# An encoder layer on one core: features-major x in the first FFN, and the weight sums of a seven-product form made partly by adding DMA transfers

## The chip, the cores and the metric

The kernel runs on one core of a Trainium2 chip. The metric is device microseconds (us) of one launch, the median of three runs. A core has TensorE (PE in the profile's rows, its weight loads PEld), VectorE (DVE), ScalarE (ACT), GpSimd (POOL) and SyncE (SP), which issues most DMA transfers. GpSimd can issue transfers too.

## What is computed

One layer of an encoder: an FFN, a token mixer (windowed attention and HGRN2), a second FFN, with a layer norm after each. There are 768 tokens (512 and 256) of 1024 features, all in float32. The two FFNs, called a and b here, are where the change lies:

```python
def swiglu_ffn(x, w13, w2):
    gate, up = jnp.split(x @ w13, 2, axis=-1)
    return (jax.nn.silu(gate) * up) @ w2
...
x = layer_norm(ALPHA * x + 0.5 * swiglu_ffn(x, ffn_w13[l, 0], ffn_w2[l, 0]), ln_g[l, 0], ln_b[l, 0])
x = layer_norm(ALPHA * x + mix, ln_g[l, 1], ln_b[l, 1])
x = layer_norm(ALPHA * x + 0.5 * swiglu_ffn(x, ffn_w13[l, 1], ffn_w2[l, 1]), ln_g[l, 2], ln_b[l, 2])
```

Each FFN has 2 x 2816 columns in w13, so 11 pairs of 256 gate columns and 11 pairs of 256 up columns.

## The kernel before

Every float32 operand of a product is split into two float32r parts, hi and lo (`split`, L111 to L113: ScalarE rounds the source to hi, VectorE subtracts hi from the source and gives lo). A product is then three matmuls: hi hi, hi lo, lo hi.

The first product of an FFN, w13 against x, is done in pairs of two 128-column tiles, by a seven-product form (a Strassen-Winograd form; the comment at L233 writes it out). The weights of a pair are four blocks A11, A12, A21, A22 (two halves of the features, two column tiles), x is four blocks B11, B12, B21, B22 (two token halves, two halves of the features). Seven products, each 4 x 3 = 12 matmuls of 384 tokens, take four sums S1 to S4 of weight blocks and four sums T1 to T4 of x blocks. S sums are made for each pair (`pair_weights`, L334), T sums once for each FFN (`form_sums`, L254).

x lies token-major in the tile `xr`. The products need it feature-major, so `turned` (L179) transposes 128 x 128 blocks on TensorE against an identity, into PSUM, and splits from there. FFN a does this for the four blocks of x (`form_base`) and for T1 to T4: 48 and 48 transposes.

The first gate pair is done in the plain form (`first_pairs`, L460 and `plain`, L466): 96 matmuls, which need only the four blocks of x, while T1 to T4 and the weights of the first up pair are made. From then on the loop at L497 goes through 11 steps of a gate pair and an up pair. Between products `fill` puts groups of six matmuls of the second product (w2, tile `pd`, L446). Their results are added to `xr` by VectorE (L450).

Buffers decide how far ahead things run. `ring` holds the split weight blocks: 6 tiles, so a block of the next pair is split as soon as a product has read one of the present pair. `raw` holds weights as they were loaded: 4 tiles, two for a pair, two for w2. SP issues loads in program order and waits at each for its tile to be free:

```python
def pair_load(w, c0, n):
    return load(col_unit(w, c0, 256, 4 * n, 4)).rearrange("p (k c) -> p k c", k=4)
```

In the order in which a scheduler puts each engine's instructions, every engine runs its own list strictly from the front: an instruction that waits holds up all behind it on that engine.

## Time and profile before

| | |
|---|---|
| median of three runs | 1485.89 us (1484.82 to 1486.19) |
| profiled execution: its span, first to last instruction (the page gives no other time of it) | 1483.4 us |
| TensorE, VectorE, ScalarE, GpSimd busy | 98%, 68%, 42%, 4% |
| instructions of TensorE / VectorE / ScalarE / GpSimd | 9439 / 1708 / 1226 / 68 |
| moved by DMA | 104.62 MB, mean 71 GB/s |
| granted TensorE clock, mean | 0.997 (of 2.4 GHz) |

A matmul's busy time overlaps that of the next one: twelve matmuls of 384 columns that each show 336 ns start 0.17 us apart. So a span of TensorE is read from starts, not from busy times. The page's percentage for TensorE tells that it hardly ever stands still, not how fast it goes.

### The profile page before, as it was taken

How to read it: one execution, taken by the hardware profiler on the slowest of the kernel's cores; microseconds unless marked ns; L12 is line 12 of the kernel's file. 1: busy time of each engine (PE TensorE's matmuls, PEld its weight loads, DVE VectorE, ACT ScalarE, POOL GpSimd, SP SyncE). 2: the span in 40 equal slices, each digit the busy share in tenths (PEclk: the TensorE clock that was granted, in tenths of full speed). 3: DMA queues.
4: the chain of work that ended last, by engine and by line, in shares of the span. 5: the costliest groups of instructions: out<-in, count | busy, mean ns of one | idle time of the engine just before them, and what ended most of it. 6: DMA issues, size and time to landing. Idle time of an engine off the chain costs nothing.

```text
span 1483.4 us, 23172 instructions
## 1 busy us (share of the span) xinstructions
PE 1454.8 (98%) x9439; PEld 1349.2 (91%) x9439; DVE 1010.3 (68%) x1708; ACT 617.3 (42%) x1226; POOL 52.7 (4%) x68
## 2 busy tenths in 40 slices
PE   8999999999999999999999999999999999999996
PEld 7999999999999888999988997899999999999995
DVE  7876677766777668444588746786777666777656
ACT  5543333333334444465664332363333324333341
POOL 1000000000000110000000001110000000000003
PEclk9999999999999999999999999999999999999999
DMA  6130222202212341211111042111212112122122
GB/s 200 58 100 31 85 77 67 85 29 86 86 57 86 105 114 44 72 30 30 29 45 44 17 142 100 43 60 54 86 57 86 56 59 86 60 84 70 45 71 86
DMA packets 86827, 104.62 MB, mean 71 GB/s; under 512 B 11816, under 2 KB 75712, under 8 KB 86720
## 3 DMA queue, kind: packets, MB, share of 16 engines
q1 hardware_dynamic: 86720, 103.14, 21.8%
q8 instruction: 74, 1.21, 0.4%
q14 instruction: 33, 0.27, 0.1%
HBM read 96.83 MB, written 6.29 MB: 70 GB/s over the span
## 4 chain that ended last, share of the span: by engine, by line
PE 89%; DVE 5%; ACT 2%; POOL 1%; issue 1%; DMA 1%; SPq 0%; DVEq 0%; ACTq 0%; POOLq 0%
PE pa L382 29%; PE pd L446 21%; PE pb L382 12%; PE pa L159 9%; PE ptm L609 5%; PE pwo L965 3%; PE pp L844 2%; PE pa L475 2%; PE ptr L183 1%; PE pav L738 1%; DVE xr L315 1%; PE plv L651 1%; ACT Ft L297 1%; PE ps L828 1%; PE pp L838 1%
## 5 line engine op out<-in xcount | busy, mean ns | idle before, releaser
L382 PE MATMUL pa<-areaA,ring 128*128 128x384 f32 x1488 | 274.1, 336 | 0.0
L382 PEld LDWEIGHTS pa<-areaA,ring 128*128 128x128 f32 x1488 | 260.8, 188 | 6.0
L113 DVE TENSOR_TENSOR ring<-raw,ring 128x512 fp32r<-128x512 f32 (+1 forms) x159 | 127.9, 807 | 88.5 <-ACT ring L112 84.6
L382 PE MATMUL pa<-areaB,ring 128*128 128x384 f32 x984 | 185.4, 337 | 0.0
L112 ACT CAST ring<-raw 128x512 fp32r<-128x512 f32 (+1 forms) x159 | 112.5, 710 | 174.7 <-PE pa L382 77.0
L446 PE MATMUL pd<-kc,Kt 128*128 128x512 f32 x720 | 185.1, 392 | 0.0
L382 PEld LDWEIGHTS pa<-areaB,ring 128*128 128x128 f32 x984 | 174.0, 188 | 6.0
L450 DVE SCALAR_TENSOR_TENSOR xr<-pd,xr 128x512 f32<-128x512 f32 x240 | 164.5, 686 | 6.2 <-PE pd L446 6.0
L159 PE MATMUL pa<-areaA,ring 128*128 128x384 f32 x864 | 167.5, 343 | 0.9 <-ACT Kt L628 0.8
L446 PEld LDWEIGHTS pd<-kc,Kt 128*128 128x128 f32 x720 | 133.7, 188 | 21.1
L159 PEld LDWEIGHTS pa<-areaA,ring 128*128 128x128 f32 x864 | 148.3, 188 | 2.5 <-ACT Kt L628 1.4
L112 ACT CAST ring<-P 128x512 fp32r<-128x512 f32 x80 | 49.8, 622 | 180.0 <-DVE Ft L352 51.2
L113 DVE TENSOR_TENSOR ring<-P,ring 128x512 fp32r<-128x512 f32 x80 | 55.3, 692 | 88.5 <-ACT ring L112 85.9
L446 PE MATMUL pd<-P,Kt 128*128 128x512 f32 x360 | 103.1, 394 | 1.0 <-DVE xr L450 1.0
L446 PE MATMUL pd<-Xt,Kt 128*128 128x512 f32 x360 | 102.4, 392 | 0.0
L382 PE MATMUL pb<-areaB,ring 128*128 128x384 f32 x480 | 91.2, 339 | 0.0
L382 PE MATMUL pb<-areaA,ring 128*128 128x384 f32 x480 | 89.8, 335 | 0.0
L382 PEld LDWEIGHTS pb<-areaB,ring 128*128 128x128 f32 x480 | 85.6, 188 | 3.1
L382 PEld LDWEIGHTS pb<-areaA,ring 128*128 128x128 f32 x480 | 84.5, 188 | 3.2
L609 PE MATMUL ptm<-ring,areaA 128*128 128x256 f32 x576 | 81.7, 289 | 0.0
L446 PEld LDWEIGHTS pd<-Xt,Kt 128*128 128x128 f32 x360 | 67.6, 188 | 15.1
L609 PEld LDWEIGHTS ptm<-ring,areaA 128*128 128x128 f32 x576 | 72.7, 191 | 0.5
(226 smaller groups left out, 2005.9 us busy)
## 6 DMA issues: line engine op xcount, KB each, us to landing
raw<-ffn_w SPq DMA_DIRECT2D x132, 512.0 KB, 4.1
raw<-w_in SPq DMA_DIRECT2D x22, 512.0 KB, 3.8
raw<-w_out SPq DMA_DIRECT2D x8, 512.0 KB, 3.4
park<-xr SPq DMA_DIRECT2D x6, 512.0 KB, 2.6
xr<-park SPq DMA_DIRECT2D x6, 512.0 KB, 6.3
raw<-w_in SPq DMA_DIRECT2D x8, 256.0 KB, 4.2
y_sample<-xr SPq DMA_DIRECT2D x4, 512.0 KB, 2.6
xr<-x_sample SPq DMA_DIRECT2D x6, 256.0 KB, 5.7
```

Of the source, the lines that this page charges most:

```text
L112: act.copy(dst_hi, src)
L113: dve.tensor_tensor(dst_lo, src, dst_hi.bitcast(F32), ALU.subtract)
L159: pe.matmul(pt, lhsT=hl[wi][:, k * P:(k + 1) * P], rhs=tri(g * 2048 + xi * 1024 + k * P), start=n == 0, stop=n == 3 * KT - 1)
L183: pe.transpose(pt[:, k * P:(k + 1) * P], src[:, k * P:(k + 1) * P], ident)
L297: act.activation(junk[c], x[c], AF.Square, bias=nm, accum_out=w[:, 2 + c:3 + c])
L382: pe.matmul(bank, lhsT=ws[b][:, wi, k, :], rhs=view(tl, off + xi * 512 + k * P, [[dist, 3], [1, P]]), start=n == 0 and not more, stop=n == ...
L446: pe.matmul(pd, lhsT=hT[f][:, hi * T + t * P:hi * T + (t + 1) * P], rhs=w[wi], start=n == 0, stop=n == tot - 1)
L450: dve.scalar_tensor_tensor(xs, pd, 0.5, xs, ALU.mult, ALU.add, accum_out=total)
L475: pe.matmul(bank, lhsT=w[:, k, m * P:(m + 1) * P], rhs=view(tl, off + xi * 512 + k * P, [[dist, 3], [1, P]]), start=i == 0, stop=i == 23)
L609: pe.matmul(pt, lhsT=xT(t, xi, k), rhs=w[k // 4][wi][:, k % 4, :], start=n == 0, stop=n == 3 * KT - 1)
L844: pe.matmul(pp[j][:, 384:448], lhsT=PTs[j % 2][:, i * P:(i + 1) * P], rhs=V[:, kb0 + i, kv * 64:kv * 64 + 64], start=i == 0, stop=i == nk - 1)
L965: pe.matmul(po[c], lhsT=cat(t, xi, k), rhs=wo[k][wi][c], start=k == 0 and n == 0, stop=k == KT - 1 and n == 2)
```

## The change

There are three parts.

**x of FFN a comes feature-major.** Besides x itself the kernel gets `x_t`, the same numbers with features on the partitions, a layout made outside (`_layouts`). `first_a` replaces `first_pairs` for FFN a. It loads x and the first weights in small steps (19 transfers ahead of all others), splits them straight from SBUF, and makes the T sums on VectorE from the untransposed blocks, 1536 elements at a time. No transposes are left in FFN a. The token-major `xr` is still loaded, for the residual, after all that. FFN b keeps `first_pairs`, `turned` and its transposes.

**Signs.** The second column tile of a pair is computed with its sign turned, so that every S sum is an addition: S1 = A21 + A22, S3 = A11 + A21, S2 = S1 + A11, S4 = S2 + A12. The T sums change sign accordingly, and the sign is undone in Silu (`scale=-1.0`) and in the product of gate and up (a multiplication by -1 within the same instruction).

**S1 and S3 by DMA.** w13 comes in another layout too (`w13_t`: for each pair and partition the blocks A22, A11, A12, A21 side by side, 2 KB each). For a pair, SP loads A22, A11, A12 into a new buffer `xb` (two tiles of 768 KB) and A22, A11 once more into a `raw` tile; GpSimd then issues two transfers that add A21 to both halves of that tile, which makes S1 and S3 in place. VectorE makes only S2 and S4. GpSimd's transfers wait for SP's load.

```diff
-    def pair_load(w, c0, n):
-        return load(col_unit(w, c0, 256, 4 * n, 4)).rearrange("p (k c) -> p k c", k=4)
-    def pair_loads(w, c0):
-        return [pair_load(w, c0, n) for n in range(2)]
+    def pair_loads(idx, j):
+        w = a["w13_t"][idx, j]
+        base = buf("xb").rearrange("p (b k c) -> p b k c", b=3, k=4)
+        nc.sync.dma_start(base, w[:, :3])
+        sums = raw_tile().rearrange("p (b k c) -> p b k c", b=2, k=4)
+        nc.sync.dma_start(sums, w[:, :2])
+        for b in range(2):
+            nc.gpsimd.dma_start(sums[:, b], w[:, 3], accum_op=ALU.add)
+        return [base[:, b] for b in range(3)] + [sums[:, b] for b in range(2)]
...
         def s2():
-            diff(1, A21, A22, ALU.add)
-            diff(2, S[1], A11)
+            S[2] = add("Dt", S1, A11)
             put(S[2])
-        def s3():
-            diff(3, A11, A21)
-            put(S[3])
         def s4():
-            diff(4, A12, S[2])
-            put(S[4])
+            put(add("P1", S[2], A12))
...
-            act.activation(G[:, 1, 384:], G[:, 1, 384:], AF.Silu)
+            act.activation(G[:, 1, 384:], G[:, 1, 384:], AF.Silu, scale=-1.0)
...
-            dve.tensor_tensor(H[:, 1, :384], G[:, 1, :384], C21, ALU.mult)
+            dve.scalar_tensor_tensor(H[:, 1, :384], C21, -1.0, G[:, 1, :384], ALU.mult, ALU.mult)
...
-        G, ws = first_pairs()
+        G, ws = first(idx, NS) if idx == 0 else first_pairs(first)
...
+    def first_a(idx, ns):
...
+        for q in range(4):
+            for k0, k1 in STEPS[q]:
+                if q < 2:
+                    for m in range(2):
+                        nc.sync.dma_start(rw[q][:, m, k0:k1], a["w13_t"][idx, 0][:, BLOCK[m][q], k0:k1])
+                nc.sync.dma_start(xb[q][:, k0:k1], a["x_t"][q // 2, q % 2][:, k0:k1])
+        ru = pair_loads(idx, ns)
+        nc.sync.dma_start(ident, a["c_ident"])
+        for t in range(NT):
+            nc.sync.dma_start(xr[:, t, :], x_rows[t])
...
+        dve.tensor_tensor(b11, b11, b12, ALU.subtract)
+        dve.tensor_tensor(b12, b22, b12, ALU.subtract)
+        dve.scalar_tensor_tensor(b22, b11, -1.0, b22, ALU.mult, ALU.subtract)
+        dve.scalar_tensor_tensor(b21, b22, -1.0, b21, ALU.mult, ALU.subtract)
+        sums(T2, b22)
+        do[2]()
+        do[3]()
+        sums(T1, b11)
...
```

How the instructions stand on two engines at the start of FFN a. TensorE first, before: `ptr` are transposes, `pa` with L475 the plain gate pair, `pa` with L382 a product of the first up pair.

```order
L183 MATMUL ptr<-ident,xr 128x128 x16
L475 MATMUL pa<-areaA,ring 128x384 x2
L183 MATMUL ptr<-ident,xr 128x128 x4
L475 MATMUL pa<-areaA,ring 128x384 x2
L183 MATMUL ptr<-ident,xr 128x128 x4
L475 MATMUL pa<-areaA,ring 128x384 x44
L183 MATMUL ptr<-ident,xr 128x128 x20
L475 MATMUL pa<-areaB_104,ring 128x384 x2
L183 MATMUL ptr<-ident,xr 128x128 x4
L382 MATMUL pa<-areaA,ring 128x384
L475 MATMUL pa<-areaB_104,ring 128x384 x11
```

The same place after the change: L593 is the plain gate pair, L384 the products of the first up pair (`areaA,ring x24`, then T1 and T2 with `kc`, T3 with `P_131`, B22 with `Xt`, T4 with `areaB_85,ring`) and, as `areaA,ring x27`, those of the next gate pair.

```order
L593 MATMUL pa<-areaA,ring 128x384 x48
L593 MATMUL pa<-areaB_85,ring 128x384 x24
L593 MATMUL pa<-areaB_84,ring 128x384 x24
L384 MATMUL pa<-areaA,ring 128x384 x24
L384 MATMUL pb<-areaA,kc 128x384
L384 MATMUL pa<-areaA,kc 128x384 x12
L384 MATMUL pb<-areaA,kc 128x384 x11
L384 MATMUL pa<-areaB_84,P_131 128x384 x12
L384 MATMUL pa<-areaA,ring 128x384
L384 MATMUL pb<-areaB_84,Xt 128x384 x12
L384 MATMUL pa<-areaA,ring 128x384 x27
L384 MATMUL pa<-areaB_85,ring 128x384 x12
```

The transposes are gone, and the product with T4 now stands behind 28 matmuls of the next gate pair.

VectorE before, behind the splits of the first blocks of x: L264 and L265 make T1 and T2 of one region, L352 the S sums, L113 the lo parts.

```order
L264 TENSOR_TENSOR Kt<-xr 128x512
L265 TENSOR_TENSOR Kt<-xr,Kt 128x512
L264 TENSOR_TENSOR Kt<-xr 128x512
L265 TENSOR_TENSOR Kt<-xr,Kt 128x512
L264 TENSOR_TENSOR Kt<-xr 128x512
L265 TENSOR_TENSOR Kt<-xr,Kt 128x512
L352 TENSOR_TENSOR Ft<-raw 128x512
L113 TENSOR_TENSOR ring<-raw,ring 128x512
L113 TENSOR_TENSOR areaB_104<-ptr,areaB_104 128x512 x3
L113 TENSOR_TENSOR areaB_103<-ptr,areaB_103 128x512 x3
L113 TENSOR_TENSOR ring<-raw,ring 128x512
L352 TENSOR_TENSOR Dt<-raw 128x512
```

After: L608 to L611 are the four T sums, L359 `Dt<-raw,xb` is S2, whose `raw` is the tile that GpSimd's transfers add to; L113 with `areaA<-Ut` is T2's lo part, with `areaA<-Kt` T1's.

```order
L608 TENSOR_TENSOR Kt<-Kt,Ft 128x1536
L113 TENSOR_TENSOR areaB_85<-Ft,areaB_85 128x2x3x128
L113 TENSOR_TENSOR areaB_84<-Ut,areaB_84 128x2x3x128 x2
L609 TENSOR_TENSOR Ft<-Ut,Ft 128x1536
L113 TENSOR_TENSOR ring<-xb,ring 128x512 x2
L610 SCALAR_TENSOR_TENSOR Ut<-Kt,Ut 128x1536
L359 TENSOR_TENSOR Dt<-raw,xb 128x512
L611 SCALAR_TENSOR_TENSOR Kt<-Ut,Kt 128x1536
L113 TENSOR_TENSOR areaA<-Ut,areaA 128x2x3x128 x2
L113 TENSOR_TENSOR kc<-Dt,kc 128x512
L113 TENSOR_TENSOR kc<-raw,kc 128x512
L113 TENSOR_TENSOR areaA<-Kt,areaA 128x2x3x128 x2
```

S2 stands ahead of everything that the products from T2 on need.

## Rows read from the trace of the kernel before

**Rows 1.** The page: busy us, share of span and instructions of each engine.

```profile
PE 1454.8 (98%) x9439; PEld 1349.2 (91%) x9439; DVE 1010.3 (68%) x1708; ACT 617.3 (42%) x1226; POOL 52.7 (4%) x68
```

**Rows 2.** Busy time by stretch: stretch, length, engines' busy us, clock, DMA share, GB/s.

```profile
0.00:10.00 10.00, 4.08 (x18) 3.74 (x19) 2.81 (x5) 4.14 (x6) 0.19 (x4) 1.00 0.79 247
10.00:20.00 10.00, 10.00 (x53) 9.81 (x52) 8.04 (x12) 4.83 (x7) 0.00 (x0) 1.00 1.07 374
30.00:40.00 10.00, 8.96 (x58) 7.93 (x57) 10.00 (x16) 8.64 (x16) 5.57 (x3) 1.00 0.22 83
50.00:60.00 10.00, 10.00 (x60) 10.00 (x59) 9.89 (x17) 4.67 (x8) 0.00 (x0) 1.00 0.43 133
100.00:200.00 100.00, 100.00 (x527) 93.64 (x526) 70.73 (x109) 38.85 (x68) 0.00 (x0) 1.00 0.24 76
```

**Rows 3.** Timeline of TensorE, first 60 us: start, us, engine, line, tiles, count.

```profile
4.94 2.79 PE L183 MATMUL ptr<-ident,xr 128*128 128x128 f32 x12 [4.94 <-DMA xr<-x_sample]
...
32.07 1.47 PE L183 MATMUL ptr<-ident,Kt 128*128 128x128 f32 x12
...
33.29 1.64 PE L382 MATMUL pa<-areaA,ring 128*128 128x384 f32 x8
...
51.58 2.24 PE L382 MATMUL pa<-areaB,ring 128*128 128x384 f32 x12
...
53.66 6.42 PE L382 MATMUL pa<-areaA,ring 128*128 128x384 f32 x36
59.92 1.55 PE L446 MATMUL pd<-kc,Kt 128*128 128x512 f32 x6
```

**Rows 4.** Timeline of SP: its first issues of x.

```profile
1.17 1.37 SPq L554 DMA_DIRECT2D xr<-x_sample  x3
```

**Rows 5.** Timeline of VectorE: one subtraction of 1024, then ones of 512 elements.

```profile
14.39 1.23 DVE L113 TENSOR_TENSOR ring<-raw,ring 128x1024 fp32r<-128x1024 f32 x1 [0.25 <-ACT ring L112]
15.54 0.68 DVE L264 TENSOR_TENSOR Kt<-xr 128x512 f32<-128x512 f32 x1
...
26.16 0.69 DVE L352 TENSOR_TENSOR Dt<-raw 128x512 f32<-128x512 f32 x1
26.76 0.69 DVE L113 TENSOR_TENSOR P<-Ft,P 128x512 fp32r<-128x512 f32 x1
```

**Rows 6.** DMA issues: tiles, count, KB each, median us from issue to landing.

```profile
raw<-ffn_w SPq DMA_DIRECT2D x132, 512.0 KB, 4.1
...
xr<-park SPq DMA_DIRECT2D x6, 512.0 KB, 6.3
...
xr<-x_sample SPq DMA_DIRECT2D x6, 256.0 KB, 5.7
...
y_prompt<-xr SPq DMA_DIRECT2D x2, 256.0 KB, 2.1
```

**Rows 7.** Timeline, an up pair: lo parts of S2, S3, A22; its first product.

```profile
64.25 0.69 DVE L113 TENSOR_TENSOR ring<-P,ring 128x512 fp32r<-128x512 f32 x1 [2.04 <-ACT ring L112]
...
71.29 0.69 DVE L113 TENSOR_TENSOR ring<-Ft,ring 128x512 fp32r<-128x512 f32 x1 [0.16 <-ACT ring L112]
...
75.48 2.36 PE L382 MATMUL pa<-areaA,ring 128*128 128x384 f32 x12
...
79.88 0.68 DVE L113 TENSOR_TENSOR ring<-raw,ring 128x512 fp32r<-128x512 f32 x1
```

**Rows 8.** Waits, whole span: who waited for whom, total us, times, longest.

```profile
DVE Dt L352 <- DMA raw<-ffn_w: 26.2, 18, 3.6
```

**Rows 9.** Start of FFN b, TensorE: a stall for the layer norm on VectorE.

```profile
961.87 0.63 PE L183 MATMUL ptr<-ident,xr 128*128 128x128 f32 x4 [0.90 <-DVE xr L315]
```

**Rows 10.** Timeline, 32 to 39 us: GpSimd's subtraction and one of VectorE.

```profile
32.75 5.57 POOL L271 TENSOR_TENSOR Kt<-xr,Kt 128x512 f32<-128x512 f32 x3 [32.32 <-PE ptr L183]
...
37.09 1.77 DVE L352 TENSOR_TENSOR P<-Dt,raw 128x512 f32<-128x512 f32 x1
```

More of the change, by code (lines that the diff above doesn't have):

```diff
@@ L403, in encoder_layer, with ffn @@
     CONST = {}
+    BLOCK = ((1, 2), (3, 0))
     W2R = ("kc", "kc", "P2", "Xt")
     ORD = (1, 2, 0, 2, 1, 0, 2, 0, 2, 0, 2)
-    def ffn(idx, ln_idx, tail, start, first=None):
-        w13 = a["ffn_w13"][0, idx]
+    def ffn(idx, ln_idx, tail, first):
         w2 = a["ffn_w2"][0, idx]
@@ L454, in weights @@
         def weights(n):
-            do, out = pair_weights(pair_loads(w13, (n % 2) * D_FF + (n // 2) * 256))
+            do, out = pair_weights(pair_loads(idx, (n % 2) * NS + n // 2))
             for f in do:
@@ L459, in weights, with first_pairs @@
             return out
-        def first_pairs():
+        def first_pairs(start):
             G = halves("Ut")
@@ L479, in plain @@
                     act.activation(G[:, m, n * 384:(n + 1) * 384], bank, AF.Silu)
-            r = first or pair_loads(w13, 0)
-            ru = pair_loads(w13, D_FF)
+            r = [raw_tile().rearrange("p (m k c) -> p m k c", m=2, k=4) for _ in range(2)]
+            for n in range(2):
+                for m in range(2):
+                    nc.sync.dma_start(r[n][:, m], a["w13_t"][idx, 0][:, BLOCK[m][n]])
+            ru = pair_loads(idx, NS)
             for b, raw in zip((B11, B21), r):
                 start(b)
-                hl.append([ring().rearrange("p (k c) -> p k c", k=4) for _ in range(2)])
+                hl.append([ring().rearrange("p (m k c) -> p m k c", m=2, k=4) for _ in range(2)])
                 split(*hl[-1], raw)
@@ L540, in ffn, with piece, put, sums @@
         finish(NT - 1)
[L543 to L558 removed]
+    def first_a(idx, ns):
+        area_b(1, F32R)
+        area_b(2, F32R)
+        rw = [raw_tile().rearrange("p (m k c) -> p m k c", m=2, k=4) for _ in range(2)]
+        G = halves("Ut")
+        xb = [buf(n) for n in ("Kt", "Kt", "Ft", "Ut")]
+        xb = [t_.rearrange("p (k c) -> p k c", k=4) for t_ in xb]
+        PLACE = (B11, B21, T4, B22)
+        STEPS = ([(0, 1), (1, 2), (2, 4)], [(0, 2), (2, 4)], [(0, 2), (2, 4)], [(0, 2), (2, 4)])
+        for q in range(4):
+            for k0, k1 in STEPS[q]:
+                if q < 2:
+                    for m in range(2):
+                        nc.sync.dma_start(rw[q][:, m, k0:k1], a["w13_t"][idx, 0][:, BLOCK[m][q], k0:k1])
[4 more added lines that the diff above has]
+            nc.sync.dma_start(xr[:, t, :], x_rows[t])
+        def piece(b, hl, k0, k1):
+            tl, off, dist = spot(b)
+            return view(tl, off + hl * 512 + k0 * P, [[P, k1 - k0], [dist, 3], [1, P]])
+        def put(b, src, k0, k1):
+            split(piece(b, 0, k0, k1), piece(b, 1, k0, k1),
+                  src[:, k0:k1].rearrange("p k (i c) -> p k i c", i=3))
+        wq = [[ring().rearrange("p (m k c) -> p m k c", m=2, k=4) for _ in range(2)] for _ in range(2)]
+        do, ws = pair_weights(ru, [None, None] + [buf(n, F32R, 1024) for n in W2R])
+        for n in range(2):
+            banks = [psa("pa")[:, :384] for _ in range(2)]
+            for q in (2 * n, 2 * n + 1):
+                b = PLACE[q]
+                tl, off, dist = spot(b)
+                hi, lo = wq[q % 2]
+                for k0, k1 in STEPS[q]:
+                    if n == 0:
+                        split(hi[:, :, k0:k1], lo[:, :, k0:k1], rw[q][:, :, k0:k1])
+                    put(b, xb[q], k0, k1)
+                    for k in range(k0, k1):
+                        for m in range(2):
+                            for i, (w, xi) in enumerate(((hi, 0), (hi, 1), (lo, 0))):
+                                pe.matmul(banks[m], lhsT=w[:, m, k, :],
+                                          rhs=view(tl, off + xi * 512 + k * P, [[dist, 3], [1, P]]),
+                                          start=q % 2 == 0 and k == 0 and i == 0,
+                                          stop=q % 2 == 1 and k == 3 and i == 2)
+            if n:
+                do[0]()
+                do[1]()
+            for m in range(2):
+                act.activation(G[:, m, n * 384:(n + 1) * 384], banks[m], AF.Silu)
+        b11, b21, b12, b22 = xb
+        def sums(b, src):
+            for k0 in (0, 2):
+                put(b, src, k0, k0 + 2)
+        dve.tensor_tensor(b11, b11, b12, ALU.subtract)
[6 more added lines that the diff above has]
+        sums(T1, b11)
+        do[4]()
+        sums(T3, b12)
+        do[5]()
+        do[6]()
+        sums(T4, b21)
+        return G, ws
```

69 lines of the change are left out of this document (32 added, 37 removed).

## The prediction

> **What bounds the kernel now.** I read the page first: TensorE is busy for 98% of the span, VectorE for 68% [rows 1]. Next the busy time by stretch, to see where that average hides something. Deep in an FFN (100 to 200 us) TensorE has no idle time and VectorE works 70.7 of 100 us; the first 60 us are another regime: TensorE works 4.08 of the first 10 us and 8.96 of those from 30 to 40, while VectorE is full, 10.0 and 9.89 of 10 [rows 2]. So deep in an FFN only fewer or shorter matmuls help, and the change has the same ones there. What it can win lies at the start of FFN a.
>
> Then the timeline of TensorE there. The first transposes start at 4.94 us, when x lands; twelve later ones fill the 1.22 us up to the next matmul, 0.10 us each; twelve matmuls of 384 columns take from 51.58 to 53.66, 0.173 us each [rows 3]. I use one mark: the start of the first group of the second product, 59.92 us [rows 3]. Ahead of it lie 96 matmuls of the plain gate pair, 84 of the first up pair and 36 of the next gate pair: 216 x 0.173 = 37.4 us. The 96 transposes are 9.8 us and the wait for x 4.9. What is left of 59.9, some 7.8 us, are waits for VectorE and slow first matmuls.
>
> **The change part by part.**
>
> *Transposes.* All 96 of FFN a go: 9.8 us of TensorE. That becomes time only as far as VectorE keeps up, so I follow both.
>
> *First data.* Three transfers of x take SP 1.37 us, 0.46 each [rows 4]; the 19 new ones are issued by 0.7 + 19 x 0.46 = 9.4 us. The first three (two of 64 KB, one of 192 KB) are out at 2.1. The first of x before was issued at 1.17 and served TensorE at 4.94, so I take the first matmul at 5.4; 216 matmuls behind it end at 42.8, the floor. The 19 transfers are 3.15 MB of x and 1.05 MB of weights. The queues moved 247 GB/s in the first 10 us and 374 in the next [rows 2]: 2.47 MB by 10 us, 4.2 MB by 14.6.
>
> *VectorE up to T2's sum.* A subtraction of 1024 starts 1.15 us before the next one, one of 512 0.60 us [rows 5]. On that line 768 take 0.87 and 1536 take 1.67. Three lo parts of 768, three T sums and two lo parts of weights (the order excerpt, L608 to L610) are 2.6 + 5.0 + 1.2 = 8.8 us. Counted from the last landing that is 23.4 us.
>
> *S1 by DMA.* Behind the 4.2 MB lie 1.31 MB of the up pair; they land by 18.1 at 374 GB/s. Then GpSimd issues its two adding transfers. No row shows such a transfer, nor any issued by GpSimd. Nearest: 256 KB took 2.1 us in quiet queues at the end and 5.7 in the full ones of the start, 512 KB behind others 6.3 [rows 6]. The residual's 3.1 MB is in the queues by then, so I take 5.7, and 0.9 for two issues at SP's pace: 18.1 + 0.9 + 5.7 = 24.7. Bounds: 18.1 + 0.45 + 2.1 = 20.7, where VectorE's 23.4 ends last instead, and 18.1 + 0.9 + 2 x 6.3 = 31.6, if each moves like 512 KB and one follows the other.
>
> *From S2 to the mark.* S2 is at the front of VectorE's list at 23.4 and waits until 24.7; queued behind it is all that the products from T2 on need. To S4's lo part VectorE has seven instructions of 512 (4.2), T4's sum (1.67) and seven lo parts of 768 (6.1): 12.0 us, so 36.7. TensorE is at T2 by about 27 and waits too. Behind S4's lo it has 10 matmuls of that product, 27 of the next gate pair, 12 with T4 and 8 more: 57 x 0.173 = 9.9, so the mark comes at 46.6. A22's, T4's second lo part and S2 of the next pair run on VectorE under those matmuls; if they didn't, T4's product would wait some 2 us. The mark moves from 59.9 to 46.6: **13.3 us** earlier.
>
> *GpSimd's subtraction for T4.* It took 5.57 us for three, and a VectorE addition within that time 1.77 us instead of 0.69 [rows 10]. It is gone in FFN a; its work is the 1.67 above.
>
> *Two S sums fewer per pair, deep in the FFNs.* 2 x 0.60 us of VectorE: worth nothing, as TensorE never waits there [rows 2]. The multiplications by -1 sit in instructions that were there. The DMA's share, 0.24 of the engines [rows 2], grows with w13, from 1.05 to 1.84 MB a pair, and stays below half. What could cost is a new wait. S2 of a pair comes right behind the lo part of S2 of the pair ahead, which ended at 64.9 in the second loop step; the `raw` tile it needs is that of two pairs earlier, free after S3's lo part, 4.2 - 0.7 us before that pair's first product (71.29 against 75.5 for the up pair), so at 50.2 where the gate pair starts at 53.66 [rows 3, 7]. The chain of load, issue and add has 64.9 - 50.2 = 14.7 us. By the rows above it takes 4.1 + 0.9 + 5.7 = 10.7. The new tile `xb` is free after A22's lo part (79.88 + 0.7, 5.1 us into a pair), at 58.8, and 768 KB at the pace of 4.1 us for 512 need 6.2: just in time. Should VectorE wait a little, it has done so before: 18 times for a load, up to 3.6 us, and TensorE did not stop [rows 2, 8]. Cost 0.
>
> *FFN b.* Its transposes stay. A stall of 0.90 us is put down to the layer norm on VectorE [rows 9]; two S sums fewer there may give back up to 1.2 us, two transfers issued between the layer norm's small instructions on GpSimd may cost up to 0.9. I take 0.
>
> **The sum.** 1483.4 - 13.3 = 1470.1 for the span. The median of the runs is 2.5 us above the profiled span, so 1485.9 - 13.3 = **1472.6 us**. A measurement of this kernel can tell 0.2%, 3 us, from no change.
>
> What the Trainium skill would say of the adding transfer stands apart: "DMA: Bandwidth & Descriptors", section "Anatomy of one DMA — SWDGE (gpsimd) path", gives 2.0 us and the bytes at 436 GB/s for a transfer issued from GpSimd, an estimate of 2.6 us for 256 KB; S1 would be there at 21.6, VectorE's 23.4 would end last, and the time would be 1471.3. Rows of full queues speak against so short a time, so the sum keeps 5.7.
>
> **The rivals.**
>
> *Late sums.* The accumulations share full queues with the residual and read what they write. At the upper bound, 31.6, the mark comes at 53.5: 6.4 us gained, 1479.5. For it: the DMA's share is 1.07 from 10 to 20 us [rows 2]. Against: those queues still moved 374 GB/s, and the adds are 0.5 MB.
>
> *GpSimd held up by VectorE.* In this kernel the two slow each other when both work: 1.77 for 0.69 us, and 1.86 us for each GpSimd subtraction [rows 10]. VectorE is without pause when GpSimd has to issue. If each issue is held as long as the longest stretched instruction, 2 x 1.77 = 3.5 us, S1 comes at 28.2 and the mark at 50.1: 9.8 gained, 1476.1. Against it: those three instructions read two tiles each, an issue reads none. The Trainium skill, "GPSIMD Engine Reference", section "1. Specifications", states the rule: GpSimd shares its access to SBUF with VectorE and contends with VectorE instructions of two SBUF inputs. The trace agrees for an arithmetic instruction; none shows an issue.
>
> *Slower: the adding transfers are slow everywhere.* The place is S2 on VectorE, in each of some 38 pairs deep in the FFNs. It decides once the chain takes longer than the 14.7 us it has and the 3.6 us that VectorE was seen to wait without harm [rows 8]: 18.3. Each us beyond costs 38 us, so 0.35 us beyond eats the gain. At 19 us, 0.7 beyond: 27 lost, 13 gained, 1500. It needs an add of 14 us where 512 KB in a row took 6.3.
>
> *Nothing gained.* VectorE was full from 30 to 60 us [rows 2], and the change leaves it about as much: what it saves on lo parts and S sums it gets back as T4's sum. If the transposes were hidden behind it, the time stays 1485.9. Against: in the first 20 us VectorE worked only 2.81 and 8.04 us [rows 2], and that idle time is what the early landing of x fills.
>
> **How the numbers follow.** Forecast 0.55, late sums 0.22, GpSimd held 0.11, nothing gained 0.04, slower 0.08. The range reaches down to the floor of TensorE, a mark of 42.8: 17.1 gained, 1468.8. Up, to 1481: the late sums' 1479.5 and 1.5 for both delays partly together. Beyond lie nothing gained and slower, 0.12, and a little of the two in between. Faster by over 0.2%: 0.55 + 0.22 + 0.11 = 0.88; within 0.2%: 0.04; slower: 0.08.
>
> **What would show it.** Right: no transposes in FFN a, the first group of the second product near 46.6 us, S2's first wait on VectorE ending near 25, and from there to the end the same intervals as before, TensorE without idle time deep in the FFNs. Wrong: an S2 that waits again in each pair with TensorE idle behind it; a mark later than 53.5; matmuls that start more than 0.173 us apart; or a stretch behind the start that is longer than before by more than 2 us.

## The result and the profile after

The changed kernel takes 1477.32 us (median of 4 runs, 1475.67 to 1478.0), the kernel before beside it 1486.04: the ratio is 0.9941, 95% interval 0.9927 to 0.9955. So it is faster by 8.7 us where 13.3 were forecast, inside the range, 4.7 us above the forecast of 1472.6. The profiled span went from 1483.4 to 1473.7 us. Of two kernels below one execution each, at 3657.71 and at 6475.19 us, lies far outside the rest and is left out of their medians.

The page of the changed kernel: the engines' busy time, the queue that GpSimd feeds (packets, MB, share of 16 engines), and the group of its issues.

```profile
PE 1443.5 (98%) x9343; PEld 1338.0 (91%) x9343; DVE 954.1 (65%) x1615; ACT 615.0 (42%) x1222; POOL 121.5 (8%) x149
...
q0 software_dynamic: 12096, 22.03, 9.6%
...
L340 POOL DMA_DIRECT2D raw<-w_t x84 | 74.4, 1038 | 792.4 <-DVE P L359 615.9
```

Against [rows 1] TensorE has 96 instructions fewer (the transposes), VectorE is busy 56 us less, and GpSimd has 84 issues of adding transfers, some 1.04 us each. By stretch, in the columns of [rows 2]:

```profile
0.00:10.00 10.00, 4.54 (x13) 3.73 (x13) 2.69 (x7) 4.44 (x7) 0.19 (x4) 1.00 0.68 199
10.00:20.00 10.00, 9.89 (x54) 9.50 (x55) 8.60 (x10) 9.01 (x13) 0.00 (x0) 1.00 1.02 403
...
30.00:40.00 10.00, 6.58 (x27) 6.32 (x28) 10.00 (x13) 8.08 (x12) 1.75 (x2) 0.83 0.83 257
100.00:200.00 100.00, 100.00 (x524) 93.36 (x523) 63.11 (x98) 36.03 (x63) 7.03 (x8) 1.00 0.38 110
```

Deep in an FFN nothing has changed for TensorE, 100 of 100, although VectorE fell from 70.7 to 63.1. The odd stretch is 30 to 40 us: TensorE works 6.58 of 10 and its mean clock is 0.83. TensorE's timeline there, as [rows 3]:

```profile
5.39 11.71 PE L593 MATMUL pa<-areaA,ring 128*128 128x384 f32 x48 [5.39 <-ACT areaA L112]
...
30.47 0.45 PE L384 MATMUL pb<-areaA,kc 128*128 128x384 f32 x1 [0.88 <-ACT kc L112]
33.87 3.75 PE L384 MATMUL pa<-areaA,kc 128*128 128x384 f32 x12 [2.95 <-ACT nr L391]
37.41 2.29 PE L384 MATMUL pb<-areaA,kc 128*128 128x384 f32 x11
...
41.80 2.28 PE L384 MATMUL pb<-areaB,Xt 128*128 128x384 f32 x12
...
52.07 0.39 PE L448 MATMUL pd<-kc,Kt 128*128 128x512 f32 x1
```

The first matmul comes at 5.39. T2's product waits 2.95 us. The mark (the start of the first group of the second product) comes at 52.07, 7.85 us earlier than in [rows 3] and 5.5 later than the forecast's 46.6. VectorE (first three rows) and GpSimd (last) say why:

```profile
23.61 1.75 DVE L610 SCALAR_TENSOR_TENSOR Ut<-Kt,Ut 128x1536 f32<-128x1536 f32 x1
28.55 0.69 DVE L359 TENSOR_TENSOR Dt<-raw,xb 128x512 f32<-128x512 f32 x1 [3.19 <-DMA raw<-w_t]
...
40.15 0.69 DVE L113 TENSOR_TENSOR Xt<-P,Xt 128x512 fp32r<-128x512 f32 x1
```

```profile
20.07 1.98 POOL L340 DMA_DIRECT2D raw<-w_t  x2 [19.64 <-DMA raw<-w_t]
```

S2, the first L359 row, waits 3.19 us for the adding transfer that makes S1. And the chain of waits between 11 and 34 us (start, us, what) shows that the second one, which makes S3, holds ScalarE as well:

```profile
11.41 8.33 DMA raw<-w_t
...
20.82 10.52 DMA raw<-w_t
...
31.36 0.02 ACT P L112
...
33.44 0.38 ACT nr L391
33.82 0.04 issue
33.87 3.75 PE pa L384 x12
```

The load that is added to was issued at 11.41 and took 8.33 us; the second adding transfer took 10.52. ScalarE's hi part of S3 (P) stood at the front of its queue, with the copy `nr`, which T2's product needs, behind it.

### The profile page after: what moved, and what is told of

It reads as the page before. It is cut to its first block, busy times and chain, and to the rows that moved or that the text cites. A ratio compares the mean times of both kernels' runs of the same rounds, so it can differ in the third digit from the quotient of the medians.

```text
span 1473.7 us, 23217 instructions
## 1 busy us (share of the span) xinstructions
PE 1443.5 (98%) x9343; PEld 1338.0 (91%) x9343; DVE 954.1 (65%) x1615; ACT 615.0 (42%) x1222; POOL 121.5 (8%) x149
## 4 chain that ended last, share of the span: by engine, by line
PE 88%; DVE 5%; ACT 2%; DMA 2%; POOL 1%; issue 1%; SPq 0%; DVEq 0%; ACTq 0%; POOLq 0%
PE pa L384 30%; PE pd L448 21%; PE pb L384 12%; PE pa L159 9%; PE ptm L672 4%; PE pwo L1028 4%; PE pp L907 2%; DMA raw<-w_t 1%; PE pav L801 1%; DVE xr L320 1%; DVE Ut L768 1%; PE ps L891 1%; ACT Ft L302 1%; PE ptr L187 1%; PE pp L901 1%
## 5 line engine op out<-in xcount | busy, mean ns | idle before, releaser
L384 PE MATMUL pa<-areaA,ring 128*128 128x384 f32 x1488 | 273.1, 335 | 0.0
L384 PEld LDWEIGHTS pa<-areaA,ring 128*128 128x128 f32 x1488 | 261.0, 188 | 6.0
L384 PE MATMUL pa<-areaB,ring 128*128 128x384 f32 x984 | 185.3, 337 | 0.0
L384 PEld LDWEIGHTS pa<-areaB,ring 128*128 128x128 f32 x984 | 174.0, 188 | 6.0
L112 ACT CAST ring<-raw 128x512 fp32r<-128x512 f32 (+2 forms) x116 | 84.6, 731 | 218.7 <-PE pb L384 92.5
L112 ACT CAST ring<-xb 128x512 fp32r<-128x512 f32 x126 | 77.9, 621 | 176.3 <-PE pa L384 130.1
L113 DVE TENSOR_TENSOR ring<-xb,ring 128x512 fp32r<-128x512 f32 x126 | 87.6, 698 | 92.7 <-ACT ring L112 90.2
L340 POOL DMA_DIRECT2D raw<-w_t x84 | 74.4, 1038 | 792.4 <-DVE P L359 615.9
L113 DVE TENSOR_TENSOR ring<-raw,ring 128x512 fp32r<-128x512 f32 (+2 forms) x116 | 96.0, 829 | 40.6 <-ACT ring L112 33.8
L384 PE MATMUL pb<-areaB,ring 128*128 128x384 f32 x480 | 91.3, 338 | 0.0
L384 PE MATMUL pb<-areaA,ring 128*128 128x384 f32 x480 | 90.1, 334 | 0.0
L384 PEld LDWEIGHTS pb<-areaB,ring 128*128 128x128 f32 x480 | 85.6, 188 | 3.1
L384 PEld LDWEIGHTS pb<-areaA,ring 128*128 128x128 f32 x480 | 84.5, 188 | 3.4
```

Of the source, the lines that this page charges most:

```text
L112: act.copy(dst_hi, src)
L113: dve.tensor_tensor(dst_lo, src, dst_hi.bitcast(F32), ALU.subtract)
L340: nc.gpsimd.dma_start(sums[:, b], w[:, 3], accum_op=ALU.add)
L384: pe.matmul(bank, lhsT=ws[b][:, wi, k, :], rhs=view(tl, off + xi * 512 + k * P, [[dist, 3], [1, P]]), start=n == 0 and not more, stop=n == ...
```

## The experiments

The theory after the result (A): all of the gain comes from the feature-major x; the adding transfers are worth nothing deep in the FFNs, and at the start they cost what the forecast lacks, because they share full queues with the residual. The rivals: an adding transfer is slow by itself; the chain of VectorE bounds the start anyway; the adds win something elsewhere. The mark depends on how the scheduler mixes the groups into the next pair, so the table has in its place the start of a matmul of the output projection that all kernels have (the first `pwo<-Ut,areaB`). The kernel before, timed beside each set of kernels, came at 1484.70 to 1486.44 us, so the ratio is to be read rather than the median; kernels whose ratios differ by 0.001 to 0.002 overlap in their intervals.

| kernel | median us | ratio to before, 95% | S2 starts | S4's lo part ends | output projection |
|---|---|---|---|---|---|
| before | 1486.04 | 1 | | | 878.04 |
| changed | 1477.32 | 0.9941, 0.9927 to 0.9955 | 28.55 | 40.84 | 869.47 |
| first sums on VectorE | 1473.88 | 0.9919, 0.9905 to 0.9932 | 29.88 | 39.99 | 867.11 |
| first sums on GpSimd | 1474.10 | 0.9925, 0.9911 to 0.9938 | 27.38 | 39.42 | 866.82 |
| late residual | 1476.93 | 0.9942, 0.9929 to 0.9954 | 25.92 | 37.97 | 870.61 |
| next pair first, then residual | 1474.05 | 0.9930, 0.9917 to 0.9943 | 26.25 | 38.47 | 866.38 |
| same, added-to load first | 1476.21 | 0.9943, 0.9929 to 0.9957 | 27.00 | 40.23 | 869.36 |
| same, and T4's sum late | 1474.29 | 0.9933, 0.9919 to 0.9947 | 26.55 | 37.55 | 866.34 |
| adding transfers alone | 1486.67 | 1.0004, 0.9995 to 1.0013 | | | 878.85 |
| no adding transfer | 1474.28 | 0.9930, 0.9917 to 0.9943 | 30.27 | 40.39 | 867.48 |
| no adding transfer, T4's sum late | 1471.61 | 0.9906, 0.9887 to 0.9925 | 27.31 | 37.62 | 865.65 |
| four adding transfers a pair | 1484.33 | 0.9999, 0.9990 to 1.0009 | 29.14 | 41.49 | 873.65 |
| filler matmuls | 1478.43 | 0.9960, 0.9947 to 0.9972 | 29.28 | 41.35 | 871.59 |

### The adding transfers alone

```
-        G, ws = first(idx, NS) if idx == 0 else first_pairs(first)
+        G, ws = first_pairs(first)
...
-    ffn(0, 0, tail_mix, first_a)
+    ffn(0, 0, tail_mix, start_a)
```

(`start_a` is that of the kernel before; `first_pairs` loads `ident` and x as the kernel before does.)

> The adding transfers and the additions alone: FFN a starts with token-major x and 96 transposes as in the kernel before. Theory A (all the gain is in FFN a's start, the adds deep in the FFNs are worth nothing): within 0.2% of the kernel before, 1484 to 1487.5. Rival 1 (the 1.9 us that the changed kernel gained behind the mark come from the adds): 1483.5 to 1484.5, and the stretch from the mark to the end some 2 us shorter than 1423.5. Rival 2 (the adds cost something deep in the FFNs, which the shorter start hid): above 1488.

The time is 1.0004 of before. Its stretch from the mark (60.71) to the end is 1484.0 - 60.71 = 1423.3 us, before 1423.5. Both rivals fall: what 84 adding transfers win or cost there lies within the interval, 0.0005 to one side and 0.0013 to the other.

### No adding transfer

In effect (the run does it in functions of its own, for every pair):

```
-        nc.sync.dma_start(sums, w[:, :2])
-        for b in range(2):
-            nc.gpsimd.dma_start(sums[:, b], w[:, 3], accum_op=ALU.add)
+        nc.sync.dma_start(sums[:, 1], w[:, 3])
...
         def s2():
+            dve.tensor_tensor(S1, A22, S3, ALU.add)
             S[2] = add("Dt", S1, A11)
...
+        def s3():
+            dve.tensor_tensor(S3, A11, S3, ALU.add)
+            put(S3)
```

> Feature-major x as in the changed kernel, but no adding transfer at all: each pair loads its four blocks once and VectorE forms S1 and S3, two instructions of 512 more a pair. Theory A (deep in the FFNs the adding transfers are worth nothing, since TensorE never waits there): the same time as the run that has VectorE's sums in the first up pair alone, 1473.9, within 1.5; VectorE back to some 70 of 100 us between 100 and 200 us, TensorE at 100. Rival 1 (the freed VectorE time is worth something, at FFN b's start if anywhere): 1475.5 or more. Rival 2 (the adding transfers cost something, by their waits or the 0.8 MB more per pair): 1472 or less.

1474.28. It doesn't separate from the kernel that has VectorE's sums in the first pair alone (1473.88; the intervals overlap), which is what theory A says of the 41 other pairs. VectorE has 68.8 of 100 us from 100 to 200 us, TensorE 100, and the mean DMA share of that stretch falls from 0.38 to 0.20. The feature-major x without any adding transfer is not slower than the change as it was made.

### The first pair's sums on VectorE, and on GpSimd

```
-        ru = pair_loads(idx, ns)
+        ru = pair_loads_v(idx, ns)
```

(`pair_loads_v` loads the fourth block plainly; S1 and S3 of this pair are formed by VectorE as in the diff above. In the second kernel `pool.tensor_tensor` forms them.)

> FFN a's first up pair loads all four weight blocks and VectorE forms S1 (just ahead of S2) and S3 (just ahead of its split); the other 41 pairs keep their adding transfers. In the changed kernel S2 waited 3.19 us for the first adding transfer and started at 28.55 us; the mark (start of the first group of the second product) came at 52.07. Theory A (the late first add cost the start 3.9 us, and TensorE's idle time before T2 brought its granted clock to the 1.2 GHz level, which cost some 1.5 us more): T2's sum is done at about 25.3, S1 takes 0.7 of VectorE, S2 starts at 26.0; the 0.7 of S3 comes back later; T2's product runs at 0.173 us a matmul; mark at 52.07 - 2.55 + 0.7 + 0.7 - 1.5 = 49.4 at most 50.2 and at least 48.7; time 1477.3 - 2 to 3.4 = 1474 to 1475.3. Theory B (VectorE's own 12 us chain is what counts, the wait at S2 would be taken up elsewhere): mark stays within 0.7 of 52.07 and the time at 1477 to 1478.

> As the run before, but GpSimd's arithmetic forms S1 and S3 of FFN a's first up pair from the loaded blocks. Theory A: the blocks land by about 18.5, GpSimd takes some 1.9 us for each addition, S1 is there at 20.5 to 22, before VectorE has T2's sum (25.3, or up to 1.5 later if the two engines slow each other); S2 starts at 25.3 to 27, VectorE has nothing to add, mark at 52.07 - 3.2 - 1.5 = 47.4, up to 48.9 with the slowing; time 1472.6 to 1474.5, the fastest of this set. Rival (VectorE slowed by GpSimd for all of the two additions): S2 at 27.5 or later, no better than the run with the sums on VectorE.

The times come where theory A put them, 1473.88 (0.12 below its range) and 1474.10. VectorE and TensorE with the sums on VectorE:

```profile
25.87 0.68 DVE L372 TENSOR_TENSOR raw<-xb,raw 128x512 f32<-128x512 f32 x1
...
29.88 0.68 DVE L367 TENSOR_TENSOR Dt<-raw,xb 128x512 f32<-128x512 f32 x1
```

```profile
31.27 0.62 PE L399 MATMUL pa<-areaA,kc 128*128 128x384 f32 x2 [1.47 <-ACT kc L112]
...
40.05 2.03 PE L399 MATMUL pb<-areaB,Xt 128*128 128x384 f32 x10 [0.76 <-DVE Xt L113]
...
49.57 0.39 PE L463 MATMUL pd<-kc,Kt 128*128 128x512 f32 x1
```

S1 is formed at 25.87. The scheduler put S2 behind T4's sum and T2's lo parts (so it starts at 29.88, later than in the changed kernel, and the forecast of 26.0 for it was wrong), but nothing waits in front of it; TensorE's wait is 1.47 instead of 2.95, and the mark comes at 49.57, 2.5 us earlier than in the changed kernel. S4's lo part gives 0.85 of that (39.99 for 40.84); the rest is TensorE, which now comes to S4's product in time: it has done two of its matmuls and waits 0.76 us for that lo part.

With GpSimd adding, S2 starts at 27.38 and the mark comes at 49.98, both later than theory A had them (27 and 48.9 at most), and the kernel is no faster than the one with VectorE's sums. VectorE's instructions beside GpSimd's were stretched:

```profile
20.28 1.53 DVE L113 TENSOR_TENSOR areaB<-Ut,areaB 128x768 fp32r<-128x768 f32 x1 [0.89 <-ACT areaB L112]
21.74 2.85 DVE L619 TENSOR_TENSOR Ft<-Ut,Ft 128x1536 f32<-128x1536 f32 x1
```

```profile
19.71 1.29 POOL L349 TENSOR_TENSOR raw<-xb,raw 128x512 f32<-128x512 f32 x1 [19.28 <-DMA raw<-w_t]
21.08 1.89 POOL L350 TENSOR_TENSOR raw<-xb,raw 128x512 f32<-128x512 f32 x1
```

1.53 and 2.85 us where the same rows take 0.96 and 1.75 in the changed kernel: 1.7 us given back, about what VectorE's two additions take in the other kernel (0.68 us each). The Trainium skill ("GPSIMD Engine Reference", section "1. Specifications") says that GpSimd shares its access to SBUF with VectorE and contends with VectorE instructions of two SBUF inputs; these rows agree. GpSimd's issues of transfers show no such stretch: in the changed kernel two take 1.75 us from 30 to 40 us, where VectorE works all 10.00 us, and 1.74 to 1.98 elsewhere in the first 60 us.

### Late residual

```
+        nc.sync.dma_start(park[0][:, :2], ru[3][:, 0, :2])
+        nc.sync.dma_start(park[0][:, 2:4], ru[4][:, 0, :2])
         for t in range(NT):
             nc.sync.dma_start(xr[:, t, :], x_rows[t])
```

> The changed kernel, with two 1 KB transfers on SP's queue that read S1 and S3, placed ahead of the six residual loads, so that these 3.1 MB (and the next pair's loads) go out only when the adding transfers are done. Theory A1 (the first adding transfer took 10.5 us because the residual filled the queues): it takes 4 to 6 us instead, S2 starts at 25.3 to 26.5, TensorE's wait before T2 shrinks and its clock stays at the upper level, mark 47.5 to 49, time 1473 to 1474.5. Theory A2 (an adding transfer is slow at this place by itself, since it reads and writes the same SBUF tile that has just landed or since GpSimd's issue is held up by VectorE): the landing stays at about 31, mark at 52, time 1477. Rival: the residual comes too late, and the scaling of it or the next pair's loads hold up the step behind: mark early, time not.

The trace's view of line 340 for the issues from 15 to 23 us gives the time to landing of the first two adding transfers, in the changed kernel and here:

```profile
DMA to landing us min/median/max: 8.5/9.5/10.5
```

```profile
DMA to landing us min/median/max: 5.4/5.6/5.9
```

That is A1: the same two transfers at the same place take 5.4 and 5.9 us when loads are held back, and 8.5 and 10.5 when they are in the queues. A2 falls. What was held back is three of the six residual loads (the other three slipped ahead of the little transfers in SP's order), the next pair's loads and two loads of the second product's weights, so the run doesn't tell the residual's share from theirs. The time did not follow, because the rival came true as well, but for its early mark: the mark came at 52.45. VectorE, TensorE, and the stretch behind (columns as in [rows 2]):

```profile
25.92 0.69 DVE L359 TENSOR_TENSOR Dt<-raw,xb 128x512 f32<-128x512 f32 x1
...
45.17 0.69 DVE L359 TENSOR_TENSOR Dt<-raw,xb 128x512 f32<-128x512 f32 x1 [4.19 <-DMA raw<-w_t]
```

```profile
49.54 3.10 PE L384 MATMUL pa<-areaA,ring 128*128 128x384 f32 x12 [3.15 <-ACT nr L391]
```

```profile
51.00:54.00 3.00, 3.00 (x11) 2.81 (x10) 3.00 (x5) 2.50 (x4) 0.00 (x0) 0.50 0.86 261
```

S2 of the first pair starts at once (25.92), S2 of the next pair waits 4.19 for its load, which now stands behind the residual; TensorE stops for 3.15 us. The wait moved by one pair.

### Next pair first, then the residual

The two loads of the next pair stand ahead of the little transfers and the residual:

```
             wu, ws = ws, (weights(2 * s + 2) if s < NS - 1 else None)
+            if late:
+                ru = late.pop()
+                for b in range(2):
+                    nc.sync.dma_start(park[0][:, 2 * b:2 * b + 2], ru[3 + b][:, 0, :2])
+                for t in range(NT):
+                    nc.sync.dma_start(xr[:, t, :], x_rows[t])
...
-        for t in range(NT):
-            nc.sync.dma_start(xr[:, t, :], x_rows[t])
+        late.append(ru)
```

> As the run with the late residual, but the next pair's two loads (1.28 MB) stand ahead of the two 1 KB transfers and the residual in SP's queue, the loads of the second product's weights behind. Expected from the run with the late residual: there S2 started at 25.9, S4's lo part ended at 38.0 and the clock did not fall before T2, but the next pair's S2 waited 4.2 us for its loads and TensorE 3.15 us. With those loads early the mark comes 9.9 behind S4's lo part, 47.9 to 48.5, 3.6 to 4.2 earlier than in the changed kernel: time 1473 to 1474. Rival: the residual lands by 36 and the second product's weights by 38 to 39, too late for ScalarE's order, and the mark stays above 50.

1474.05, the upper end of what was expected; the mark is 0.6 later than expected, and the output projection starts 3.1 us earlier than in the changed kernel. S2 starts at 26.25 and waits 0.71. So with the adding transfers kept, the order of the loads alone gives back some 3 us by the traces and the medians, 1.6 by the ratios, whose intervals overlap. No load of the residual was issued ahead of 26.6 us here, and the first two adding transfers, with the next pair's loads in the queues, took:

```profile
DMA to landing us min/median/max: 6.1/6.1/6.2
```

TensorE at S4's product, and the mark:

```profile
38.65 2.24 PE L384 MATMUL pb<-areaB,Xt 128*128 128x384 f32 x12
...
49.10 0.39 PE L449 MATMUL pd<-kc,Kt 128*128 128x512 f32 x1
```

### Added-to load first, and T4's sum late

```
+        nc.sync.dma_start(sums, w[:, :2])
         nc.sync.dma_start(base, w[:, :3])
-        nc.sync.dma_start(sums, w[:, :2])
...
-        dve.scalar_tensor_tensor(b21, b22, -1.0, b21, ALU.mult, ALU.subtract)
         sums(T2, b22)
...
         do[5]()
-        do[6]()
+        dve.scalar_tensor_tensor(b21, b22, -1.0, b21, ALU.mult, ALU.subtract)
         sums(T4, b21)
+        do[6]()
```

(The first kernel has the first part alone.)

> The run with the next pair's loads first, and in every pair the load that is added to (512 KB) stands ahead of the load of the three plain blocks (768 KB). In the run before, GpSimd waited until 20.1 us for that load of the first up pair and S2 started at 26.25, 0.7 behind VectorE's free moment. Expected: the 768 KB fall out of the way, some 1.9 us at 400 GB/s, the adds are issued at about 18.2, S1 is there before 25.4, S2 starts when VectorE is free (25.4 to 25.6); mark 0.7 earlier than 49.1, time 0.7 less than 1474.05. Rival: A11 and A12, needed by VectorE at 22.6, now come late instead, and nothing is gained or some is lost.

> The run before, and T4's sum (1.75 us of VectorE, three columns of instructions ahead of T2's lo part) is formed behind S4, since T4 is the last operand that the up pair needs. VectorE is full from 15.4 us to the mark, so if its order is what bounds the mark now, T2's product starts 1.5 to 2 us earlier, S4's lo part 1.5 us earlier, and the mark comes at 46.5 to 47.5, which is what the prediction had for the changed kernel; time 1471.5 to 1473. Rival: TensorE then waits for T4's lo part instead (its product is the last of the up pair), or ScalarE's scaling of the residual stands in the way; time no better than 1473.4.

The first is no faster than the kernel it was made from: its median is 2.2 us above (the intervals of the two ratios overlap), and its output projection starts 3.0 us later. The load landed earlier (GpSimd issues at 18.86), S1 was there in time, but the scheduler, with the load ahead, set S3's hi part further forward in ScalarE's order, and there it waited for the second adding transfer, with T2's hi parts behind it:

```profile
26.34 0.62 ACT L112 CAST P<-raw 128x512 fp32r<-128x512 f32 x1 [2.13 <-DMA raw<-w_t]
...
28.87 1.57 ACT L112 CAST areaA<-Ut 128x768 fp32r<-128x768 f32 x2
```

S2 started at 27.00 with no wait in front of it: a lo part of T1 now stands ahead of it on VectorE, whose work before that also ran some 0.7 us later in this execution. With T4's sum late the same wait of ScalarE is there (2.15 us), and what VectorE's order wins only makes up for it: 1474.29. S4's lo part was done at 37.55, but TensorE, which had started T2's product no earlier (32.76 for 32.93), came to S4's product behind that and waited there for a copy on ScalarE:

```profile
39.05 2.35 PE L384 MATMUL pb<-areaB,Xt 128*128 128x384 f32 x12 [0.40 <-ACT qt L397]
```

So the forecast of 1471.5 to 1473 failed on ScalarE, not on VectorE.

### No adding transfer, T4's sum late

> The run without any adding transfer (1474.28), with T4's sum formed behind S4 as in the run before. VectorE has two sums more before S4's lo part (1.4 us), so if the adding transfers are of use at all, it is here: 1.0 to 1.5 us slower than the run before (1472.5 to 1474.5). If it is as fast or faster, the adding transfers are worth nothing even where VectorE bounds the time.

> The kernel of the run before once more (no adding transfer, T4's sum behind S4), for its rows: the profiled execution of the first time shows another speed than the timed ones and can't be read. Expected: 1472.9 within 0.8; the mark about 1.4 us earlier than with VectorE's sums in the first up pair alone and T4's sum early (49.57), so near 48.2; TensorE's wait before T2's product below 1.3 us and its clock at 1.00. If the time comes at 1474 or more, it is no better than the other versions.

The first took 1472.82 (0.9919, 0.9906 to 0.9932), the second 1471.61, somewhat below what was expected. The kernel has the lowest time of the table, clear of the changed kernel but not of the one with the first sums on VectorE (interval 0.9905 to 0.9932), and it holds no adding transfer: ScalarE has no wait from 24 to 40 us, and TensorE runs on at the start without the wait of 2.95 us:

```profile
30.39 0.62 PE L399 MATMUL pa<-areaA,kc 128*128 128x384 f32 x2
30.85 0.33 PE L399 MATMUL pb<-areaA,kc 128*128 128x384 f32 x1
31.25 2.01 PE L399 MATMUL pa<-areaA,kc 128*128 128x384 f32 x10
```

It was expected to be slower than the run with adding transfers and T4's sum late (1474.29), and isn't: the two additions of 0.6 us cost no more than waiting for the transfers. That run has ScalarE's wait of 2.15 us for a transfer, so the pair doesn't show what an adding transfer is worth where VectorE alone bounds the time. (The mark came later than expected, at 50.55, but with the next pair's matmuls ahead of it; the output projection is 3.8 us earlier than in the changed kernel.)

### Four adding transfers a pair

```
-        for b in range(2):
+        for b in (0, 1) if idx == 0 and j == NF // 2 else (0, 1, 0, 1):
             nc.gpsimd.dma_start(sums[:, b], w[:, 3], accum_op=ALU.add)
```

> The changed kernel with four adding transfers in each pair instead of two (the block is added twice; FFN a's first up pair keeps two), the second round behind the first: S1 and S3 hold the block twice, a part of the computation that is changed. It measures how much room the chain load - issue - add has deep in the FFNs. By the prediction's terms the chain has 14.7 us and took 10.7; the second round adds 0.96 x 2 + 5.6, so 18 us, 3.5 beyond. If VectorE's spare time absorbs that (it has waited 3.6 us without harm): S2 waits in most pairs, TensorE not, time within 0.2% of the changed kernel, 1475 to 1480. If the room is less: TensorE waits in each pair, 1 us a pair is 40 us, above 1490. If the room is more than the prediction had: hardly a wait at S2, time 1477.

1484.33, 7 us above the changed kernel, all that the change had gained (0.9999 of before) and above what was expected, but far from 40 us. (Its profiled execution was the fastest of twelve, 1481.30, so the rows show some 5 us of this.) The group of S2 in the changed kernel, then here (mean ns of one behind the busy time, then idle time before):

```profile
L359 DVE TENSOR_TENSOR Dt<-raw,xb 128x512 f32<-128x512 f32 x42 | 29.0, 690 | 4.4 <-DMA raw<-w_t 3.2
```

```profile
L359 DVE TENSOR_TENSOR Dt<-raw,xb 128x512 f32<-128x512 f32 x42 | 29.0, 691 | 62.0 <-DMA raw<-w_t 61.4
```

```profile
63.94 1.66 PE L448 MATMUL pd<-kc,Kt 128*128 128x512 f32 x6 [3.22 <-DVE xr L452]
```

With four, S2 waits 21 times, up to 3.9 us, and TensorE still works 100 of 100 us deep in the FFNs; one stop is new, 3.22 us in the first loop step. The output projection starts 4.2 us later; what the 7 us are made of beyond that stop no row shows. With two, S2 waits for a transfer in one pair of 42. So two transfers have the room that the prediction gave them, and even four, which do cost, stay far from the rival's 1 us in each pair.

### Filler matmuls

```
+                if idx == 0 and s == 0 and n == B21:
+                    bank = psd("pdf")[:, :384]
+                    for i in range(FILL):
+                        pe.matmul(bank, lhsT=wu[B21][:, 0, i % 4, :], rhs=tri(1024 + i % 4 * P),
+                                  start=i == 0, stop=i == FILL - 1)
```

> The changed kernel with 22 matmuls of 384 columns on an unused PSUM bank between the second and the third product of FFN a's first up pair (nothing reads them), so that TensorE works through most of the 2.95 us in which it waited for T2's operands. Nothing else moves: S2 still waits for the first adding transfer until about 28.6. Theory C (the other part of the shortfall is the clock: after that wait the granted clock was at the 1.2 GHz level, and T2's twelve matmuls took 3.54 us instead of 2.08): the clock stays at 1.00, T2's product takes 2.1 us, mark 52.07 - 1.46 = 50.6, time 1477.3 - 1.5 = 1475.9. Rival (VectorE and ScalarE are behind anyway, so a faster T2 product only waits later, at S4's lo part, which ended at 40.84): T2's product is faster and the mark is not earlier than 51.7; time 1477.3. Second rival: the fillers delay T2's first matmul and the time gets worse.

The granted clock first, in the changed kernel, behind the 2.95 us in which TensorE stood (columns as in [rows 2]):

```profile
34.00:35.00 1.00, 1.00 (x5) 1.00 (x6) 1.00 (x2) 1.00 (x2) 0.91 (x2) 0.72 0.81 332
35.00:36.00 1.00, 1.00 (x5) 1.00 (x4) 1.00 (x2) 1.00 (x2) 0.83 (x1) 0.50 0.27 64
```

0.50 is the 1.2 GHz level; T2's twelve matmuls take 37.41 - 33.87 = 3.54 us. With the fillers the clock stays at 1.00 and they take 2.2:

```profile
34.61 2.35 PE L384 MATMUL pa<-areaA,kc 128*128 128x384 f32 x12 [0.74 <-ACT nr L391]
36.80 2.25 PE L384 MATMUL pb<-areaA,kc 128*128 128x384 f32 x12
40.87 2.35 PE L384 MATMUL pa<-areaB,P 128*128 128x384 f32 x12 [1.82 <-ACT qt L395]
```

So the clock fell because TensorE stood. The time is no better (1478.43), but the run doesn't settle the price: the scheduler put the copy `qt` behind four scalings of the residual on ScalarE, and T3's product waited 1.82 for it. From the changed kernel's own rows there is a bound: TensorE came to S4's product at 41.80, S4's lo part was done at 40.15 + 0.69 = 40.84, 0.96 earlier. With a full clock it would also have had two of S4's matmuls done ahead of that lo part, as with the first sums on VectorE, so the clock cost at most 0.96 + 2 x 0.173 = 1.3 us.

## Why the prediction was right, and where it was off

**Transposes, first data.** Right: 96 transposes gone, first matmul at 5.39 for 5.4. VectorE had T2's sum at 25.4 (23.61 + 1.75), 2.0 later than forecast, without effect, as S1 came later still. The runs show that the gain is that of the new start: with the old start 1.0004, with the new one and no adding transfer 0.9930. What x in its new layout, the 19 small loads and the T sums on VectorE each give was not separated.

**S1 by DMA.** This is the term that was mis-sized: 24.7 forecast, 28.55 measured, 3.85 us late. Half of it is the load ahead: "they land by 18.1" became 11.41 + 8.33 = 19.74, and GpSimd's first issue came at 20.07; in the first 10 us the queues moved 199 GB/s where 247 were taken from [rows 2]. The other half is the transfer: 0.9 + 5.7 = 6.6 us forecast, 8.5 measured from the issue. The 5.7 was chosen from [rows 6] as a value of full queues; the run with the late residual shows 5.4 and 5.9 for two such transfers with those loads held back, against 8.5 and 10.5 with them. The rival of late sums had the mechanism; the result lies between it and the forecast. That SP's other loads are the cause of the transfer's part is shown by that run and by the one with the next pair first (6.1 and 6.2); how much of it is the residual and how much the loads of the second product's weights, held back with it, is not. The load's part stays open: SP's 19 issues ended at 10.51 where 9.4 was forecast, and with the residual behind the next pair's loads GpSimd's first issue came no earlier, at 20.08; with the added-to load first, at 18.86.

The Trainium skill's rule ("DMA: Bandwidth & Descriptors", section "Anatomy of one DMA — SWDGE (gpsimd) path"), 2.0 us and the bytes at 436 GB/s, gives an estimate of 2.6 us for 256 KB. No adding transfer here was that short: the least of 84 took 4.1 us, the median 5.6. The measurement decides.

**ScalarE was left out.** The prediction followed VectorE and TensorE. The chain of waits runs through ScalarE, where S3's hi part waited for the second adding transfer ahead of `nr`. VectorE's own delay would have brought T2's product at about the same time (S2's lo part ended at 32.57 + 0.68 = 33.25, the product started at 33.87), so this made 0.6 us here, or some 1.0 if two of the product's matmuls could have gone ahead of that lo part, as they do in the kernel without adding transfers and T4's sum late. In the run with the added-to load first ScalarE waited 2.13 us in the same way, and nothing of the earlier load was left.

**From S2 to the mark.** 12.0 us to S4's lo part were right: 40.84 - 28.55 = 12.3. From there 9.9 were forecast and 11.2 measured, and this is TensorE being late: after the wait and T2's matmuls at the 1.2 GHz level it came to S4's product 0.96 behind the lo part, and with all 12 of its matmuls still to do where the prediction had 10. From there to the mark 59 matmuls take 52.07 - 41.80 = 10.27 us, 0.174 each, as forecast. The prediction counted T2's twelve at 0.173 as well; they took 3.54 / 12 = 0.295.

**The sum of the misses.** 3.85 + 0.3 + 1.3 = 5.5 us, the whole distance of the mark.

**Deep in the FFNs, nothing.** Right, and shown from both sides: with the adds alone 1.0004; without any 0.9930, beside 0.9919 with them in all pairs but the first. "Slower" fell: S2 waits for a transfer in one pair of 42. The rival "GpSimd held up by VectorE" fell: 0.85 to 1.25 us an issue, and 1.75 for two where VectorE worked without pause. "Nothing gained" fell with the mark.

**Its own signs.** Of the signs of being right, the transposes and TensorE's work deep in the FFNs came as said; the mark (52.07 for 46.6), S2's wait (28.55 for 25) and the stretch behind did not. One sign of being wrong came: matmuls more than 0.173 us apart, T2's. So the place and the mechanism of the gain were right, and the time is inside the range because the range reached up to late sums, which came in part.

**Behind the mark.** Forecast 0; the stretch is 1.9 us shorter. Some 0.7 lie ahead of the output projection's start, where the first group now stands mixed with the next pair's matmuls; 1.1 lie behind it (605.4 before, 604.2 after). The places, first before, then after:

```profile
904.33 3.90 PE L965 MATMUL pwo<-ring,areaB 128*128 128x512 f32 x9 [2.12 <-ACT pwo L297]
```

```profile
894.57 2.37 PE L1028 MATMUL pwo<-ring,areaB 128*128 128x512 f32 x9 [0.90 <-ACT pwo L302]
...
899.11 1.06 PE L187 MATMUL ptr<-ident,xr 128*128 128x128 f32 x8 [0.76 <-DVE xr L320]
```

The stall at the second layer norm is shorter and no half clock follows. Nothing ties it to the change: over the kernels of the table the stretch behind the projection's start is 604.0 to 605.7 us, and this stall is 1.97 with the adding transfers alone and 1.97 without any. What sets it from kernel to kernel stays open.

**Median and span.** The forecast added 2.5 us to the span, here the median is 3.6 above it (the profiled execution was the fastest of the four). 5.5 - 1.9 + 1.1 = 4.7, the miss of the time. That the 1.9 made it smaller is luck.

## What to carry to other kernels

A transfer that adds in DMA is no free instruction: its chain is load, wait, issue, transfer, and each consumer, on every engine's queue, stands behind it. Where the engine that it relieves is not the bound it won nothing here, and at the start, where all loads leave at once, it cost some 3 us. Order the loads by when they are needed, and leave what is needed late (here 3.1 MB of residual) behind them: that was worth as much as taking the adding transfers away (0.9930 each). If an in-order engine has spare time, as VectorE had here, add there.
